# Second layer of an encoder trunk: two column blocks in the wide product form, and another timetable for the modulation sums

## The chip, the cores and the metric

The kernel runs on one core of one Trainium2 chip. The metric is the device time of one execution in microseconds (us); the time of a kernel is the median of its runs. Engines are called as the profile calls them: PE is TensorE's matmul, PEld its weight load, DVE is VectorE, ACT is ScalarE, POOL is GpSimd and SP is SyncE, which here only issues DMAs.

## What is computed

Two layers of a bidirectional encoder over one sequence of 256 tokens and 2048 features. Each layer is a parallel pair of attentions behind one input projection, one output projection, and a dense squared-ReLU MLP. Every sub-layer is modulated by a conditioning vector. Cut to what matters here:

```python
cond = silu(c)
for l in range(2):
    mod = cond @ w_ada[l] + b_ada[l]              # 2048 x 12288: six vectors of 2048
    sh_a, sc_a, g_a, sh_m, sc_m, g_m = split(mod, 6)
    h = rmsnorm(x) * (1 + sc_a) + sh_a
    proj = h @ w_in[l]                            # dq, dk, dv, cq, ckv, kr
    out_a = diff_attention(dq, dk, dv, ...)       # 4 heads, two score maps each
    q  = rmsnorm(cq, q_norm_g[l]) @ w_uq[l]       # latent queries, 512 wide
    kv = rmsnorm(ckv, kv_norm_g[l]) @ w_ukv[l]    # latent keys/values, 256 wide
    out_b = mla_attention(q, kv, rope(kr))        # 8 heads
    x = x + g_a * (concat(out_a, out_b) @ w_o[l])
    h = rmsnorm(x) * (1 + sc_m) + sh_m
    x = x + g_m * (square(relu(h @ w_mlp_in[l])) @ w_mlp_out[l])
return rmsnorm(x, final_norm_g)
```

## The kernel before

**Products.** Nearly every product is computed on two rounded parts of each operand, `hi` and `lo = value - hi`, both 32-bit "fp32r", as hi·hi + hi·lo + lo·hi. Activations are held transposed, a tile of 128 features by 256 tokens for each of the 16 k-tiles of `h`. Weights come in "raw" tiles of 128x2048 floats (1 MB) over SP's queue into a ring of five buffers (`raw`, L170). `weights` (L136) then makes two halves of each: ACT copies a half to `hi` (L151) and DVE subtracts to get `lo` (L154), each into a ring of four 128x1024 buffers.

There are two forms of the product of one weight tile (128x128) with one k-tile of `h`, called a unit here:

- the narrow form, `mac` (L191): three matmuls of 256 columns, weights hi, hi, lo (lines 194, 197, 198). `tile_cols` (L200) does a whole column tile of 16 units that way, `by_k` (L247) a block of tiles k by k, where several output banks stay open.
- the wide form: the hi and lo parts of `h` lie side by side, so that one matmul of 512 columns does hi·hi and hi·lo in the two halves of a bank, and one matmul of 256 columns adds lo·hi. `wides` (L207) does a pair of column tiles: all hi matmuls of both tiles (L217), then all lo matmuls of both (L220). `wide_by_k` (L265) does it k by k with open banks (L281 lo, L284 hi); at k = 0 it takes the lo matmul first. The two halves of a bank have then to be added: `joined` (L1344) calls `join` (L1350) for each of two banks, one ACT copy of 256 columns (L1351) and one DVE multiply-add (L1352), where the narrow form needs one ACT copy of 512 columns (`copy`, L344).

**The modulation sums.** `mod = cond @ w_ada` isn't done on PE. The matrix comes in 192 tiles of 1 MB over the same SP queue and the same five `raw` buffers (`ada_load`, L361), and DVE multiplies each tile with `cond` and adds along the row in one instruction (`ada_sums`, L375, L380), followed every second tile by an add of the bias (L392 or L394). When they are done is a timetable: each call of `weights` ends in `more_ada` (L159), which first issues the sums of tiles loaded since, behind that call's last `lo`, then adds `self.rate` to a credit and issues one load for each whole unit of credit. The rate is set by stage: constants `RATE_...` at L98. So a load issued in one call of `weights` has its sum in the next call. What a stage needs at the latest is done by force (`ada_need`). The last group, `g_m` of layer 1, is needed by `gate(1, 5)` (L1255) behind the first of the four blocks of the last MLP.

**The second layer's attention** (`layer`, L867, with `l = 1`): `norm_then_by_k` (L729) makes `h` and, with it, the six latent column tiles (cq, ckv) in `wide_by_k`, six banks open. Then, in the order of the code: the `w_d` block (four tiles: first diff-attention key head, last query head) by `by_k` in two banks `later`; six query tiles `w_q1` in three calls of `wides`; the latent keys' norm (`latent`, L713: squares on ACT, row sums and spread on PE, scale and split); copies of the two `later` banks to `kk` and `q`; the rope keys (`keys`, one narrow tile); six key tiles `w_t` by `tile_cols`, one by one (`col`, L909), with the latent queries' norm after the first of them and the scores of heads 0 to 2 (`probs`) between; then `up_r`, `up_k`, `up_q` (products with the latents, narrow), `up_v`, eight value blocks (`val`) between the eight MLA heads, and the output projection `w_o`.

**The last MLP** (`block_by_seven`, L1065): for each of four blocks of 2048 hidden features, a loop over pairs `m` of column tiles. Each pair is two single wide tiles, joined, through squared ReLU and split; from the third pair of a block on, each pair also runs two steps of an earlier pair (`seven`, L1133: `five` and `two`), products by sums and differences of weight blocks that DVE makes (L1164 to L1166, then L154). In block 0 the first six tiles were made with the norm, so the loop starts at m = 6. Steps that are left run after the loop; then the rest of the output columns (`rows_by_k`, L311 to L314).

The order of the instructions on each engine is made by the framework's scheduler from the order of the code, its dependences and its own cost estimates; `behind` fixes an order where the author wants one.

Of the kernel before, what the change touches and what calls it, by code (L numbers as in the profile page):

```python
# [16 lines left out]
P = 128  # L17
T = 256
D = 2048
NK = D // P  # L20
# [30 lines left out]
V_QG = 196  # L51
# [43 lines left out]
WHOLE = 6  # L95


RATE_A0, RATE_V, RATE_A1, RATE_A2, RATE_K, RATE_K1, RATE_M = 1.1, 1.6, 0.5, 0.7, 0.6, 0.0, 0.7  # L98
FILL = "0|1|2|3||||rlm"


class Trunk:
# [607 lines left out]
            ins = nc.vector.scalar_tensor_tensor(lo, t[:, i], sh[:, c], hi.bitcast(F32), ALU.add, ALU.subtract)  # L710
        return out, ins

    def latent(self, vals, g):  # L713

        nc = self.nc
        acc = None
        for v in vals:
            acc = self.sumsq(acc, v)
        r = self.rstd(acc, 2 * P * len(vals))
        out = []  # L720
        for b, v in enumerate(vals):
            t = self.t("lt")
            for i in range(2):
                k = 2 * b + i
                nc.vector.scalar_tensor_tensor(t[:, i], v[:, i], g[:, k : k + 1], r, ALU.mult, ALU.mult)
            out += self.split(t, "lat")
        return out
# [139 lines left out]
    def layer(self, l, acc=None):  # L867
        nc, io = self.nc, self.io
        qs = 1.0 / math.sqrt(128.0)
        ms = 1.0 / math.sqrt(192.0)  # L870
        fill = self.fills() if l == 0 else []
        later = []

        def next_by_k(kqs):
            def f(h, whole=()):
                if not later:
                    later.extend(self.open_banks(2))
                for kq in kqs:
                    f32 = whole if 4 * kq + 4 <= len(whole) else None
                    blocks = self.by_k_weights([io["w_d"][l, kq]], 4, f32)  # L880
                    self.by_k(later, blocks, h, 4 * kq, NK, 4, f32)
            return f

        if l == 0:
            early = {p: next_by_k(kqs) for p, kqs in EARLY.items()}
            h, banks = self.first_norm_then_by_k(acc, io["w_a"], 3, fill, early)
        else:
            self.rate = RATE_K1
            h, banks = self.norm_then_by_k(l, 0, 1, io["w_a1"])
            nc.gpsimd.dma_start(self.row, self.bias_kept)  # L890
        done = sum(len(k) for k in EARLY.values()) if l == 0 else 0
        self.rate = RATE_A0 if l == 0 else RATE_A1
        if l == 0:
            cqr = [self.copy(ps, "cqr") for ps in banks[:2]]
            ckr = self.copy(banks[2], "ckr")
        else:
            cqr = [self.joined(banks[i : i + 2], self.u("cqr")) for i in (0, 2)]
            ckr = self.joined(banks[4:], self.u("ckr"))
        q = []
        cq, ckv = [], []  # L900
        kk, qn, kn, qr, vm, a, at, v, o = [], [], [], [], [], [], [], [], []
        self.mo = []

        def keys():
            ps = self.bank("pkr")
            self.tile_cols(ps[:, 0], io["w_kr"][l], h)
            self.kr = (self.rope_k_parts if l else self.rope_k)(ps[:, 0])

        def col(i, out, scale):  # L909
            def f():  # L910
                if i % 2 == 0:
                    self.ps = self.bank("ps")
                self.tile_cols(self.ps[:, i % 2], io["w_t"][l, i], h)
                if i % 2:
                    out.append(self.copy(self.ps, "k", scale))
            return f
# [21 lines left out]
        def val(cg, kq):  # L938
            def f():
                if kq == 0:  # L940
                    self.pv = [self.bank("pv") for _ in range(2)]
                w = self.weights(io["w_dv"][l, cg, kq])
                w = [[z[:, 512 * j : 512 * j + 512] for z in y] for y in w for j in range(2)]
                self.tokens_by_k(self.pv, w, h[4 * kq : 4 * kq + 4], kq == 0, kq == 3)
                if kq == 3:
                    v.append([self.copy(ps, "v").rearrange("p a b -> p (a b)") for ps in self.pv])
            return f

        def probs(hd):
            return lambda: a.append(self.diff_probs(l, hd, q[hd], kk[hd]))  # L950
# [7 lines left out]
        for i in range(HM + 2):  # L958
            for s in range(3):
                if 0 <= i - s < HM:  # L960
                    mla.append(heads[i - s][s])
        next_by_k(range(done, 4))(h)
        if l == 0:
            q += [self.copy(ps, "q", qs) for ps in banks[3:]]
        else:
            for i in range(0, 6, 2):
                q.append(self.joined(self.wides([io["w_q1"][i + j] for j in range(2)], h), self.u("q"), qs))
        ckv += self.latent([ckr], self.vec[:, V_KVG + 2 * l : V_KVG + 2 * l + 2])
        kk.append(self.copy(later[0], "k", -1.0))
        q.append(self.copy(later[1], "q", qs))  # L970
        keys()
        order = [(0, kk, -1.0), (2, kk, -1.0), (4, kk, -1.0)]
        for n, (i, dst, scale) in enumerate(order):
            col(i, dst, scale)()
            if n == 0:
                cq += self.latent(cqr, self.vec[:, V_QG + 4 * l : V_QG + 4 * l + 4])
            probs(n)()
            col(i + 1, dst, scale)()
        if l:
            self.rate = RATE_A2  # L980
        vals = [val(cg, kq) for cg in range(2) for kq in range(4)]
        if l:
            up_r()
# [19 lines left out]
        turn(3)()  # L1003
        for f in mla[3:6]:
            f()
        if l == 0:
            self.rate = RATE_V
        self.interleave(
            vals,
            mla[6:] + [av[0][0], av[1][0]],  # L1010
        )
        if l == 0:
            self.rate = RATE_A0
        self.gate(l, 2)
        pss = [self.bank("pr") for _ in range(2)]
        self.rows_by_k(pss, self.weights(io["w_o"][l, 0, 0]), self.mo, 0)
# [14 lines left out]
        h, banks = self.norm_then_by_k(l, 3, 4, io["w_m0"] if l == 0 else io["w_m01"])  # L1031
# [613 lines left out]
```

## Time and profile before

| | |
|---|---|
| median of 3 runs | 2152.89 us (2151.78 to 2153.81) |
| profiled execution, its own time | 2149.43 us |
| span of its instructions | 2147.6 us |
| busy PE / PEld / DVE / ACT | 2119.8 / 1839.3 / 1776.0 / 1209.4 us |
| mean granted PE clock | 0.999 |
| second layer's attention, by the trace | about 1085 to 1444 us |
| its stretch from `w_d` to the last `w_t` tile | 1147.23 to 1251.74 us |
| last MLP, block 0, loop and remaining steps | 1482.9 to 1563.1 us |

The profile shows one execution of this kernel. The times that it gives lie inside the span; the profiled execution's own time is 1.8 us longer than the span. A matmul's duration in a row includes its way through the array and overlaps with the next one: what a matmul costs in a stream is the distance from its start to the next start. "Busy" is the time in which at least one instruction of that engine was under way.

### The profile page before, as it was taken

How to read it: one execution, taken by the hardware profiler on the slowest of the kernel's cores; microseconds unless marked ns; L12 is line 12 of the kernel's file. 1: busy time of each engine (PE TensorE's matmuls, PEld its weight loads, DVE VectorE, ACT ScalarE, POOL GpSimd, SP SyncE). 2: the span in 40 equal slices, each digit the busy share in tenths (PEclk: the TensorE clock that was granted, in tenths of full speed). 3: DMA queues.
4: the chain of work that ended last, by engine and by line, in shares of the span. 5: the costliest groups of instructions: out<-in, count | busy, mean ns of one | idle time of the engine just before them, and what ended most of it. 6: DMA issues, size and time to landing. Idle time of an engine off the chain costs nothing.

```text
span 2147.6 us, 29565 instructions
## 1 busy us (share of the span) xinstructions
PE 2119.8 (99%) x11411; PEld 1839.3 (86%) x11411; DVE 1776.0 (83%) x2444; ACT 1209.4 (56%) x1829; POOL 6.2 (0%) x18
## 2 busy tenths in 40 slices
PE   7999999999999999999999999999999999999998
PEld 5899888898888888888889998888888888888886
DVE  7889888988688888888877886778977897897897
ACT  6555663565465355345455576647645765664674
POOL 0000000000000000000000000000000000000000
PEclk9999999999999999999999999999999999999999
DMA  9998899799888988988967776775665564565553
GB/s 384 423 354 329 318 360 356 280 335 346 320 320 327 345 320 324 340 299 332 343 222 275 255 254 237 273 252 208 230 237 181 189 241 152 199 232 177 191 191 128
DMA packets 87245, 594.76 MB, mean 277 GB/s; under 512 B 9856, under 2 KB 10304, under 8 KB 20288
## 3 DMA queue, kind: packets, MB, share of 16 engines
q1 hardware_dynamic: 85968, 587.08, 73.8%
q0 software_dynamic: 848, 5.28, 0.6%
q8 instruction: 89, 1.46, 0.3%
q10 hardware_dynamic: 288, 0.52, 0.1%
q14 instruction: 52, 0.43, 0.1%
HBM read 589.66 MB, written 3.18 MB: 276 GB/s over the span
## 4 chain that ended last, share of the span: by engine, by line
PE 94%; DVE 3%; ACT 2%; DMA 1%; issue 1%; SPq 0%; ACTq 0%; DVEq 0%
PE ps L217 19%; PE pr L311 11%; PE pr L312 11%; PE pr L314 11%; PE ps L220 10%; PE pk L260 3%; PE pk L284 2%; PE pk L194 2%; PE pk L198 2%; PE pk L197 2%; PE pp L1156 2%; PE pp L1155 2%; PE pp L1157 2%; PE pv L298 2%; PE pv L296 2%; PE pv L297 2%
## 5 line engine op out<-in xcount | busy, mean ns | idle before, releaser
L151 ACT ACTIVATE hi<-raw 128x1024 fp32r<-128x1024 f32 (+2 forms) x714 | 719.7, 1019 | 617.1 <-PE pr L312 262.7
L154 DVE TENSOR_TENSOR lo<-raw,hi 128x1024 fp32r<-128x1024 f32 (+2 forms) x714 | 821.3, 1172 | 261.7 <-issue 104.8
L380 DVE SCALAR_TENSOR_TENSOR ada<-ada,cond 128x2048 f32<-128x2048 f32 x192 | 438.2, 2285 | 12.3 <-DMA ada<-in_w_ada 11.8
L217 PE MATMUL ps<-h,hi 128*128 128x512 f32 x1856 | 436.5, 390 | 0.0
L217 PEld LDWEIGHTS ps<-h,hi 128*128 128x128 f32 x1856 | 345.2, 188 | 71.0 <-DVE sum L1352 1.3
L311 PE MATMUL pr<-hi,hid 128*128 128x512 f32 x768 | 298.9, 389 | 0.0
L312 PE MATMUL pr<-hi,hid 128*128 128x512 f32 x768 | 298.8, 389 | 0.0
L220 PEld LDWEIGHTS ps<-h,lo 128*128 128x128 f32 x1856 | 234.1, 191 | 6.8
L220 PE MATMUL ps<-h,lo 128*128 128x256 f32 x1856 | 236.2, 283 | 0.0
L314 PE MATMUL pr<-lo,hid 128*128 128x512 f32 x768 | 190.3, 389 | 0.0
L314 PEld LDWEIGHTS pr<-lo,hid 128*128 128x128 f32 x768 | 144.2, 188 | 29.9
L311 PEld LDWEIGHTS pr<-hi,hid 128*128 128x128 f32 x768 | 144.2, 188 | 29.9
L312 PEld LDWEIGHTS pr<-hi,hid 128*128 128x128 f32 x768 | 144.2, 188 | 29.8
L1351 ACT ACTIVATE sum<-ps 128x256 f32<-128x256 f32 x110 | 41.9, 382 | 87.1 <-PE ps L220 86.2
L194 PE MATMUL pk<-h,hi 128*128 128x256 f32 x320 | 90.4, 285 | 0.2 <-ACT h L705 0.2
L198 PE MATMUL pk<-h,lo 128*128 128x256 f32 x320 | 90.5, 283 | 0.0
L197 PE MATMUL pk<-h,hi 128*128 128x256 f32 x320 | 90.5, 283 | 0.0
L260 PE MATMUL pk<-hf,w 128*128 128x256 f32 x384 | 84.1, 379 | 0.0
L260 PEld LDWEIGHTS pk<-hf,w 128*128 128x128 f32 x384 | 72.6, 190 | 10.4 <-ACT hf L677 0.6
L154 DVE TENSOR_TENSOR lo<-comb,hi 128x1024 fp32r<-128x1024 f32 x58 | 70.5, 1220 | 6.3 <-PE ps L220 6.3
L151 ACT ACTIVATE hi<-comb 128x1024 fp32r<-128x1024 f32 x58 | 60.7, 1053 | 8.5 <-PE pp L1157 5.5
L194 PEld LDWEIGHTS pk<-h,hi 128*128 128x128 f32 x320 | 61.2, 192 | 0.6 <-ACT h L705 0.5
(288 smaller groups left out, 3125.2 us busy)
## 6 DMA issues: line engine op xcount, KB each, us to landing
raw<-in_w_m SPq DMA_DIRECT2D x206, 1024.0 KB, 5.7
ada<-in_w_ada SPq DMA_DIRECT2D x192, 1024.0 KB, 6.2
raw<-in_w_o SPq DMA_DIRECT2D x32, 1024.0 KB, 5.8
raw<-in_w_ms SPq DMA_DIRECT2D x32, 1024.0 KB, 5.0
raw<-in_w_m SPq DMA_DIRECT2D x24, 768.0 KB, 5.1
raw<-in_w_dv SPq DMA_DIRECT2D x16, 1024.0 KB, 6.2
raw<-in_w_t SPq DMA_DIRECT2D x12, 1024.0 KB, 5.0
w<-in_w_a SPq DMA_DIRECT2D x24, 384.0 KB, 13.5
```

The costliest lines, as they stand in the source:

```text
L151: ins = self.nc.scalar.activation(hi, v, AF.Copy)
L154: ins = self.nc.vector.tensor_tensor(lo, v, hi.bitcast(F32), ALU.subtract)
L194: ins = mm(ps, hi, x[0], start=first, stop=False, skip_group_check=shared)
L197: mm(ps, hi, x[1], start=False, stop=False, skip_group_check=shared)
L198: self.last_mac = mm(ps, lo, x[0], start=False, stop=last, skip_group_check=shared)
L217: mm(ps.rearrange("p a b -> p (a b)"), part(w, k, 0), x[2], start=k == 0, stop=False)
L220: mm(ps[:, 0], part(w, k, 1), x[0], start=False, stop=k == nk - 1)
L260: self.nc.tensor.matmul(ps, v, whole[k], start=first, stop=last, skip_group_check=True)
L311: mm(ps, xh[:, c], part(i, 0), start=kq == 0 and i == 0, stop=False)
L312: mm(ps, xl[:, c], part(i, 0), start=False, stop=False)
L314: self.last_mm = mm(ps, xh[:, c], part(i, 1), start=False, stop=kq == 3 and i == 3)
L380: ins = nc.vector.scalar_tensor_tensor(w, w, 1.0, self.cond, ALU.mult, ALU.mult, accum_out=acc[:, i : i + 1])
```

## The change

Six edits, all for the second layer, whose core is shown below. (1) The `w_d` block goes behind the three `w_q1` pairs and takes `wide_by_k` over four open banks instead of `by_k` over two; its results are made by `joined`. (2) The six `w_t` tiles are done in pairs by `wides` and `joined`: `col(i)` does both tiles of a pair when `i` is even, and nothing when it is odd. (3) The squares and their sum for the latent queries' norm are split from `latent` into `squared` and issued ahead of `keys()`. (4) The rate of the modulation loads is 0.7 (was 0.5) for `w_q1` and `w_d`, 0.25 (was 0.5) for `keys` and `w_t`, 0 (was 0.7) for the `up_` products and the first value block, 1.0 (was 0.7) for the other seven value blocks and 0.6 (was 0.7) for `w_o`. The rates of the first layer, of the norms and of the MLPs stay as they are.

```diff
-RATE_A0, RATE_V, RATE_A1, RATE_A2, RATE_K, RATE_K1, RATE_M = 1.1, 1.6, 0.5, 0.7, 0.6, 0.0, 0.7
+RATE_A0, RATE_V, RATE_K, RATE_M = 1.1, 1.6, 0.6, 0.7
+RATE_K1, RATE_A1, RATE_C1, RATE_V1, RATE_O1 = 0.0, 0.7, 0.25, 1.0, 0.6
...
-    def latent(self, vals, g):
-
-        nc = self.nc
+    def squared(self, vals):
         acc = None
         for v in vals:
             acc = self.sumsq(acc, v)
-        r = self.rstd(acc, 2 * P * len(vals))
+        return acc
+
+    def latent(self, vals, g, acc=None):
+
+        nc = self.nc
+        r = self.rstd(acc or self.squared(vals), 2 * P * len(vals))
...
         def col(i, out, scale):
             def f():
+                if l:
+                    if i % 2 == 0:
+                        ps = self.wides([io["w_t"][l, i + j] for j in range(2)], h)
+                        out.append(self.joined(ps, self.u("k"), scale))
+                    return
...
-        next_by_k(range(done, 4))(h)
         if l == 0:
+            next_by_k(range(done, 4))(h)
             q += [self.copy(ps, "q", qs) for ps in banks[3:]]
         else:
             for i in range(0, 6, 2):
                 q.append(self.joined(self.wides([io["w_q1"][i + j] for j in range(2)], h), self.u("q"), qs))
+            later = self.open_banks(4)
+            for kq in range(4):
+                self.wide_by_k(later, self.by_k_weights([io["w_d"][l, kq]], 4, None), h, 4 * kq, NK)
         ckv += self.latent([ckr], self.vec[:, V_KVG + 2 * l : V_KVG + 2 * l + 2])
-        kk.append(self.copy(later[0], "k", -1.0))
-        q.append(self.copy(later[1], "q", qs))
+        if l == 0:
+            kk.append(self.copy(later[0], "k", -1.0))
+            q.append(self.copy(later[1], "q", qs))
+        else:
+            kk.append(self.joined(later[:2], self.u("k"), -1.0))
+            q.append(self.joined(later[2:], self.u("q"), qs))
+        acc = None
+        if l:
+            self.rate = RATE_C1
+            acc = self.squared(cqr)
         keys()
...
             if n == 0:
-                cq += self.latent(cqr, self.vec[:, V_QG + 4 * l : V_QG + 4 * l + 4])
+                cq += self.latent(cqr, self.vec[:, V_QG + 4 * l : V_QG + 4 * l + 4], acc)
             probs(n)()
             col(i + 1, dst, scale)()
         if l:
-            self.rate = RATE_A2
+            self.rate = 0.0
...
-        if l == 0:
-            self.rate = RATE_V
+        self.rate = RATE_V1 if l else RATE_V
         self.interleave(
...
-        if l == 0:
-            self.rate = RATE_A0
+        self.rate = RATE_O1 if l else RATE_A0
```

## Prediction, made before the changed kernel ran

> **What bounds the kernel now.** I read the page first, then its chain of waits, then the busy time by stretch, then the order of time.
>
> ```profile
> span 2147.6 us, 29565 instructions
> PE 2119.8 (99%) x11411; PEld 1839.3 (86%) x11411; DVE 1776.0 (83%) x2444; ACT 1209.4 (56%) x1829; POOL 6.2 (0%) x18
> PE 94%; DVE 3%; ACT 2%; DMA 1%; issue 1%; SPq 0%; ACTq 0%; DVEq 0%
> ```
>
> PE is busy for 99% of the span, and 94% of the chain that ends last is PE. So a change gains what it takes from PE's own stream, and loses whatever makes PE wait. Both have to be looked for in their stages.
>
> ```profile
> core 0: us, PE busy (x) PEld busy (x) DVE busy (x) ACT busy (x) POOL busy (x), PEclk, DMA share, GB/s
> 1147.23:1170.27 23.04, 23.04 (x195) 23.04 (x194) 16.02 (x19) 9.60 (x14) 0.00 (x0) 1.00 0.80 292
> 1170.27:1203.61 33.34, 33.34 (x195) 29.53 (x194) 21.23 (x24) 16.25 (x19) 0.00 (x0) 1.00 0.74 263
> 1210.69:1251.74 41.05, 41.05 (x327) 40.42 (x325) 36.41 (x77) 23.74 (x45) 0.00 (x0) 1.00 0.67 235
> ```
>
> These are `w_d` (narrow), `w_q1` (wide) and `w_t` (narrow) in the second layer's attention. PE never pauses in them, at full granted clock. So no wait is there to be removed: the edits can gain by a cheaper stream alone. DVE is at 70%, 64% and 89%.
>
> **The wide form: what it takes from PE.** The price of a matmul in a stream is the distance between starts.
>
> ```profile
> 1147.23 0.28 PE L194 MATMUL pk<-h,hi 128*128 128x256 f32 x1
> 1147.35 0.28 PE L197 MATMUL pk<-h,hi 128*128 128x256 f32 x1
> 1147.47 0.28 PE L198 MATMUL pk<-h,lo 128*128 128x256 f32 x1
> 1147.59 0.28 PE L194 MATMUL pk<-h,hi 128*128 128x256 f32 x1
> ...
> 1170.27 7.44 PE L217 MATMUL ps<-h,hi 128*128 128x512 f32 x32
> 1177.55 3.63 PE L220 MATMUL ps<-h,lo 128*128 128x256 f32 x29
> ...
> 1122.03 1.55 PE L284 MATMUL pk<-h,hi 128*128 128x512 f32 x6
> 1123.41 0.88 PE L281 MATMUL pk<-h,lo 128*128 128x256 f32 x6
> 1124.13 0.40 PE L284 MATMUL pk<-h,hi 128*128 128x512 f32 x1
> ```
>
> A narrow unit is three matmuls 0.12 us apart, 0.36 us; the 192 of `w_d` fill their 23.04 us exactly at that pace. In `wides`, 32 matmuls of 512 columns take 1177.55 - 1170.27 = 7.28 us, 0.2275 each; with 0.12 for the one of 256 columns a unit is 0.3475. (All 96 units of `w_q1`: 33.34 / 96 = 0.347.) In `wide_by_k`, six units take 1124.13 - 1122.03 = 2.10 us, 0.350 each. So the edit that looks like a third fewer matmuls saves 10 to 12.5 ns a unit. The six `w_t` tiles are 96 units: 96 x 0.0125 = 1.2 us. `w_d` is 64 units by `wide_by_k`: 64 x 0.010 = 0.6 us (0.8 at the pace of `wides`). Together 1.8 us off PE.
>
> The Trainium skill, page "TensorE: Matmul & The Clock Gate", section "Back-to-back issue gap", speaks against even that: a warm matmul of N columns follows the one before by N / 2.4 + 2.5 ns, so that three of 256 (328 ns) cost what one of 512 and one of 256 do (325 ns). By that rule the 160 units would save 0.4 us, and the sum below would be 4.9 instead of 3.5. The rows contradict it at 256 columns, with 120 ns, and the rows are used.
>
> **What else the attention part adds.**
>
> ```profile
> L1351 ACT ACTIVATE sum<-ps 128x256 f32<-128x256 f32 x110 | 41.9, 382 | 87.1 <-PE ps L220 86.2
> L1352 DVE SCALAR_TENSOR_TENSOR sum<-ps,sum 128x256 f32<-128x256 f32 x10 | 4.2, 418 | 0.1
> L346 ACT ACTIVATE k<-ps x6: 570/578/581, 179.2 to 1252.8; 128x512 f32<-128x512 f32 x6
> L154 DVE TENSOR_TENSOR lo<-raw,hi 128x1024 fp32r<-128x1024 f32 x27 | 32.5, 1219 | 4.7 <-ACT hi L151 4.7
> L380 DVE SCALAR_TENSOR_TENSOR ada<-ada,cond 128x2048 f32<-128x2048 f32 x192 | 438.2, 2285 | 12.3 <-DMA ada<-in_w_ada 11.8
> ```
>
> Five results are joined instead of copied: each is two ACT copies of 0.38 for one of 0.58 (+0.9 us of ACT in all) and two DVE additions of 0.42 (+4.2 us of DVE). By the timetable (below) `w_t` and `keys` lose two modulation sums of 2.29 us, so DVE there goes from 36.41 by -4.6 + 2.5 to about 34.3 of some 39.8 us; `w_q1` with `w_d` goes from 37.25 by +4.6 + 1.7 to 43.5 of some 55.8. Both stay below PE, and I cost the joins at nothing. If that cover were gone, it would be 0.84 us a join.
>
> The moves: `w_d`'s four loads pass `w_q1`'s six on SP's queue, all of 1 MB into the same ring, so nothing is late by it. The squares of the latent queries (two ACT squares, one DVE addition) go ahead of `keys`; PE's row sums that wait for them come behind a whole pair, 11.1 us, and cost nothing more than before. `probs(1)` and `probs(2)` find their keys a pair earlier. One place is tight: in a pair the `lo` buffers come free only with the second half of the stream (1177.55 + 8 x 0.12 = 1178.5, 8.2 us into 11.1), and `wide_by_k` starts with a `lo`. A subtraction of 1.22 ends at 9.5 if DVE is free and at 11.8 behind a sum: 0 to 0.7 us, once. I take 0, because in the wide stretch above DVE is free for a third of the time.
>
> **The timetable: what moves where.** Counting the calls of `weights` through the first layer (27 at 1.1, 8 at 1.6, 14 at 0.6, 114 at 0.7) gives 130.7, so the second layer starts with a credit of 0.7; the trace has 30 loads left then, two of them in the MLP:
>
> ```profile
> L364 SPq DMA_DIRECT2D ada<-in_w_ada x30: 327/328/328, 1129.7 to 1475.9; - x30
> L364 SPq DMA_DIRECT2D ada<-in_w_ada x2: 327/328/328, 1469.0 to 1475.9; - x2
> ```
>
> The count agrees: 0.7 + 17 x 0.5 + 27 x 0.7 = 28.1, so 28 in the attention. With the new rates: 0.7 + 10 x 0.7 + 7 x 0.25 + 6 x 0 + 7 x 1.0 + 14 x 0.6 = 24.85, so 24, and six are left for the MLP. There the credit runs 0.85 + 0.7n: loads at calls 1, 2, 4, 5, 6 and 8, sums at calls 2, 3, 5, 6, 7 and 9, where they were at 3 and 4. Calls 2 to 9 are the second tile of m = 6 to the first of m = 14, all in block 0's loop. The attention is relieved of four sums where PE didn't wait anyway, and the MLP gets four more. What is DVE's room there?
>
> ```profile
> 1484.60:1492.50 7.90, 7.90 (x46) 6.90 (x45) 5.93 (x13) 7.56 (x16) 0.00 (x0) 1.00 0.43 140
> 1492.50:1525.90 33.40, 33.40 (x190) 29.35 (x189) 32.76 (x54) 24.37 (x40) 0.00 (x0) 1.00 0.65 251
> 1525.90:1549.00 23.10, 23.10 (x122) 19.88 (x121) 21.91 (x30) 15.75 (x22) 0.00 (x0) 1.00 0.40 143
> 1549.00:1563.10 14.10, 14.05 (x70) 11.32 (x69) 14.07 (x21) 11.29 (x18) 0.50 (x1) 1.00 0.82 292
> ```
>
> Hardly any. From the place of call 2's sum to the end of the loop's products DVE works 5.93 + 32.76 + 21.91 + 14.07 = 74.67 of 78.5 us: 3.83 idle. And in the chain of waits that stretch isn't PE's:
>
> ```profile
> 1524.88 0.97 PE ps L220 x8
> ...
> 1525.94 1.23 DVE lo L154
> ...
> 1557.68 1.15 DVE lo L154
> 1558.87 0.50 PE pp L1156
> ```
>
> From 1525.94 to 1558.87 the chain runs through DVE alone but for 1.5 us of ACT and some issue, and where it hands back, PE has begun to wait:
>
> ```profile
> PEld pp L1156 <- DVE lo L154: 0.5, 1, 0.5
> ```
>
> So the lead that DVE had is used up at the end of the loop, and what is added before comes out as PE's wait. Four sums are 4 x 2.29 = 9.16 us; against 3.83 of idle time 5.3 us are over. Bounds: if all sums ahead of 1525.9 go into lead that PE doesn't miss, only call 9's is left, 2.3; if none of the idle time can be filled, 9.2. I take 5.3, as DVE's idle pieces lie at both ends of the sums' places. Behind the sums on DVE's queue stand the subtractions for PE's next tiles and for `five` and `two`; PE waits for those.
>
> **Sum.** -1.8 + 5.3 = +3.5 us, with its own range of 2.3 - 1.8 = +0.5 to 9.2 - 1.8 = +7.4. The rows are from the profiled execution, 2149.43 us, which is 3.46 below the median of the runs; it would become 2152.9, and the median 2152.89 + 3.5 = 2156.4 (2153.4 to 2160.3).
>
> **Rivals.** First, only the saving: the scheduler lets a sum wait while other work is ready, and DVE's work spreads beyond the loop, where it has 40.45 of 55.9 us busy:
>
> ```profile
> 1563.10:1619.00 55.90, 55.90 (x248) 46.31 (x247) 40.45 (x46) 22.61 (x22) 0.55 (x1) 1.00 0.66 244
> ```
>
> Then -1.8, 2151.1. For it: two sums stood in that loop before, and PE had one wait of 0.5. Against it: the steps' own differences and subtractions can't be put off, since the products behind them close the block.
>
> Second, clearly slower: the ring of five raw buffers. A modulation tile holds its buffer from its load to the end of its sum:
>
> ```profile
> 1475.91 0.33 SPq L364 DMA_DIRECT2D ada<-in_w_ada  x1
> 1498.77 2.28 DVE L380 SCALAR_TENSOR_TENSOR ada<-ada,cond 128x2048 f32<-128x2048 f32 x1
> DMA to landing us min/median/max: 4.7/5.3/10.2
> ```
>
> That was 25 us. Two held at a time leave three buffers for two tiles, a step's blocks and their differences per pair. It decides when a weight tile's load is issued less than 5.3 + 1.22 us and ACT's conversion before PE wants it; then a landing of 5.3 comes on top: +8.8, 2161.7. Against it: a late DVE also gives the loads time.
>
> Third, the wide form gives nothing, if PEld, full in the narrow stretch (23.04 of 23.04), is no limit there and the distance is only the form of the stream: +5.3, 2158.2. Against it stand 96 wide units at 0.347; this is also the case nearest to the skill's rule.
>
> **How the numbers follow.** Forecast 0.50, only the saving 0.25, the ring 0.15, no gain of the form 0.06, something that none of these rows shows and that is faster 0.04. About 0.2% (4.3 us) is what a measurement of this kernel can tell from no change. The saving alone lies within it; of the forecast's own range I put 0.33 within and 0.17 beyond; ring and no gain lie beyond. So faster 0.04, same 0.58, slower 0.38. The range goes from 2150.3, just below the saving alone, to 2160.3, the forecast's upper bound, and leaves out the ring and the unknown.
>
> **What would show it.** Right: `w_d` takes 22.4 and three `w_t` pairs 33.3 us without their inserts; six modulation loads after 1424 instead of two; DVE without idle time from about 1490 to the loop's end and that loop some 5 us longer, with PE's waits on `lo` (L154). Wrong: a loop as long as before with six sums in it, PE waits in `w_q1` or `w_d`, or a pace of units other than 0.35.

## The result, and the profile after

The changed kernel takes 2159.34 us (median of 9 runs, 2157.08 to 2161.39) against 2152.16 for the kernel before (9 runs): ratio 1.0034, 95% interval 1.0025 to 1.0043. That is 7.2 us slower (5.4 to 9.3), where 3.5 slower was forecast. The profiled execution of the changed kernel took 2159.23 us.

The head of its page, to be read against the first fence of the prediction:

```profile
span 2157.2 us, 29275 instructions
PE 2121.5 (98%) x11251; PEld 1830.5 (85%) x11251; DVE 1780.8 (83%) x2454; ACT 1208.7 (56%) x1834; POOL 6.2 (0%) x18
PE 90%; DVE 5%; ACT 2%; DMA 2%; issue 1%; SPq 0%; ACTq 0%; DVEq 0%
```

PE has 160 matmuls less, one for each of the 160 units, but four points less of the chain are PE's. The busy time by stretch says where. First the kernel before, from its norm to the first `up_` product, from there to the last MLP, and block 0's loop to its last `pp` product:

```profile
1147.23:1251.74 104.51, 104.51 (x771) 100.07 (x769) 80.14 (x129) 52.78 (x84) 0.00 (x0) 1.00 0.74 261
1251.74:1482.90 231.16, 230.92 (x1224) 199.14 (x1222) 174.78 (x266) 143.53 (x260) 1.05 (x2) 1.00 0.71 251
1482.90:1562.87 79.97, 79.92 (x428) 68.66 (x426) 75.55 (x115) 59.83 (x95) 0.50 (x1) 1.00 0.59 219
```

The same three stretches of the changed kernel, with `w_q1` and `w_d` by themselves ahead (after the length come PE, PEld, DVE, ACT and POOL busy, the granted clock, the DMA share and GB/s):

```profile
1149.09:1182.43 33.34, 33.34 (x194) 29.52 (x193) 25.68 (x33) 16.68 (x25) 0.00 (x0) 1.00 0.80 290
1182.43:1204.88 22.45, 22.45 (x130) 19.63 (x129) 17.78 (x18) 8.09 (x9) 0.00 (x0) 1.00 0.92 343
...
1149.09:1251.67 102.58, 102.58 (x611) 91.50 (x609) 82.19 (x128) 52.10 (x83) 0.00 (x0) 1.00 0.73 265
1251.67:1483.05 231.38, 231.14 (x1224) 199.23 (x1222) 168.33 (x267) 143.88 (x266) 1.05 (x2) 1.00 0.67 233
1483.05:1572.01 88.96, 83.37 (x429) 69.36 (x427) 84.70 (x126) 59.79 (x95) 1.05 (x2) 0.98 0.69 242
```

The stretch with the edits is 1.93 us shorter, without a pause of PE. The middle, from the `up_` products to the MLP, is 0.22 longer. The loop is 8.99 us longer: DVE works 9.15 us more in it, and its idle time is what it was, 88.96 - 84.70 = 4.26 against 79.97 - 75.55 = 4.42. The rest from the loop's end is 0.46 longer (2157.2 - 1572.01 against 2147.6 - 1562.87). The changed kernel enters the first stretch 1.86 us later, though none of the edits acts before there; that is a difference between two executions (over the first 100 us the granted clock is 0.95 in the one and 1.00 in the other). The five terms make the 9.60 between the spans; without the 1.86 they make 7.74, which goes with the 7.2 of the medians.

What the changed kernel's PE and PEld wait for in the loop, from the list of waits (total, times, longest):

```profile
PE pp L1174 <- DVE lo L155: 3.8, 5, 1.5
PE pp L1173 <- ACT hi L152: 1.6, 1, 1.6
PEld pp L1174 <- DVE lo L155: 6.2, 7, 1.9
PEld pp L1173 <- ACT hi L152: 2.6, 2, 2.1
```

And the chain of waits there, in order of time:

```profile
1503.56 1.93 PE ps L221 x16
1506.35 1.13 DVE comb L1182
...
1516.25 2.21 DVE ada L381 x2
...
1522.27 2.21 DVE ada L381 x2
...
1531.15 0.50 PE pp L1174
...
1543.98 1.14 DVE comb L1182
...
1548.07 1.14 DVE lo L155
1549.25 0.51 PE pp L1174
```

From 1505.5 on the chain runs through DVE, now with modulation sums (L381) in it, and where PE picks it up, at 1531.15 and 1549.25, it comes out of a wait. (In the changed kernel L154 has become L155, L1155 and L1156 are L1173 and L1174, and L1164 is L1182.)

### The profile page after: what moved, and what is told of

Same layout as the page of the kernel before. It is cut to its first block, busy times and chain, and to the rows that moved or that the text cites. A ratio compares the mean times of both kernels' runs of the same rounds, so it can differ in the third digit from the quotient of the medians.

```text
span 2157.2 us, 29275 instructions
## 1 busy us (share of the span) xinstructions
PE 2121.5 (98%) x11251; PEld 1830.5 (85%) x11251; DVE 1780.8 (83%) x2454; ACT 1208.7 (56%) x1834; POOL 6.2 (0%) x18
## 4 chain that ended last, share of the span: by engine, by line
PE 90%; DVE 5%; ACT 2%; DMA 2%; issue 1%; SPq 0%; ACTq 0%; DVEq 0%
PE ps L218 19%; PE pr L312 10%; PE pr L315 10%; PE pr L313 10%; PE ps L221 10%; PE pk L261 3%; PE pk L285 3%; PE pp L1174 2%; PE pp L1175 2%; PE pp L1173 2%; PE pv L299 2%; PE pv L297 2%; PE pv L298 2%; PE pk L195 1%; PE pk L199 1%; PE pk L282 1%
## 5 line engine op out<-in xcount | busy, mean ns | idle before, releaser
L155 DVE TENSOR_TENSOR lo<-raw,hi 128x1024 fp32r<-128x1024 f32 (+2 forms) x714 | 821.4, 1172 | 269.2 <-issue 108.1
L218 PE MATMUL ps<-h,hi 128*128 128x512 f32 x1952 | 459.8, 390 | 0.0
L381 DVE SCALAR_TENSOR_TENSOR ada<-ada,cond 128x2048 f32<-128x2048 f32 x192 | 438.1, 2284 | 11.8 <-DMA ada<-in_w_ada 11.3
L218 PEld LDWEIGHTS ps<-h,hi 128*128 128x128 f32 x1952 | 363.4, 188 | 75.0 <-DVE sum L1370 1.3
L221 PEld LDWEIGHTS ps<-h,lo 128*128 128x128 f32 x1952 | 246.1, 191 | 7.0
L221 PE MATMUL ps<-h,lo 128*128 128x256 f32 x1952 | 248.2, 283 | 0.0
L155 DVE TENSOR_TENSOR lo<-comb,hi 128x1024 fp32r<-128x1024 f32 x58 | 70.4, 1220 | 5.8 <-PE ps L221 5.8
L195 PE MATMUL pk<-h,hi 128*128 128x256 f32 x256 | 72.3, 285 | 0.2 <-ACT h L706 0.2
L199 PE MATMUL pk<-h,lo 128*128 128x256 f32 x256 | 72.4, 283 | 0.0
L198 PE MATMUL pk<-h,hi 128*128 128x256 f32 x256 | 72.4, 283 | 0.0
L285 PE MATMUL pk<-h,hi 128*128 128x512 f32 x256 | 67.6, 394 | 0.0
```

Of the source, the lines that this page charges most:

```text
L155: ins = self.nc.vector.tensor_tensor(lo, v, hi.bitcast(F32), ALU.subtract)
L195: ins = mm(ps, hi, x[0], start=first, stop=False, skip_group_check=shared)
L199: self.last_mac = mm(ps, lo, x[0], start=False, stop=last, skip_group_check=shared)
L218: mm(ps.rearrange("p a b -> p (a b)"), part(w, k, 0), x[2], start=k == 0, stop=False)
L221: mm(ps[:, 0], part(w, k, 1), x[0], start=False, stop=k == nk - 1)
L285: ins = mm(ps, part(j, 0), both, start=False, stop=False, skip_group_check=True)
```

## The experiments

In what follows "loop" is the third stretch above. Its end is a little loose: the scheduler puts some row products (`rows_by_k`), 0.23 us each, ahead of the last `pp` product, none before, one in the changed kernel, three in some kernels below. Counted on to the next block's first tile, the loop is 140.03 before and 148.80 in the changed kernel, 8.77 more; the expectations from "All sums early" to "Number or place" and the one of the last experiment count it so. All medians stand beside the median of the kernel before in the same job. A ratio can differ from the quotient of the two medians by up to 0.0004.

**The wide form without its timetable.** The changed kernel with the old rates:

```diff
-RATE_K1, RATE_A1, RATE_C1, RATE_V1, RATE_O1 = 0.0, 0.7, 0.25, 1.0, 0.6
+RATE_K1, RATE_A1, RATE_C1, RATE_V1, RATE_O1 = 0.0, 0.5, 0.5, 0.7, 0.7
...
-            self.rate = 0.0
+            self.rate = 0.7
```

> The changed kernel with the old rates (0.5 up to the last key tile, 0.7 from there): wide form and earlier squares alone, two modulation sums left for the last MLP. Theory 'DVE time' (the loss is the DVE time of four more sums in block 0 of the last MLP, the gain is the cheaper PE stream): 1.9 us below the kernel before, block 0 as long as before (80 us from its first tile to its row products), the stretch from the first query tile to the last key tile 102.6 us. Theory 'raw ring' (the loss comes from buffers held by modulation tiles): the same here. If the wide form itself were to blame for any of the loss, this kernel would be above the kernel before.

2152.52 us (11 runs) against 2152.07, ratio 1.0006 (0.9997 to 1.0015): not the gain of 1.9. The stretch is 102.60 long and the loop 79.95, as expected; the gain is lost between them. By stretch and by PE's waits between 1250 and 1300:

```profile
1250.78:1483.93 233.15, 231.81 (x1224) 199.25 (x1223) 178.75 (x281) 144.09 (x266) 1.05 (x2) 1.00 0.71 254
```

```profile
PE pv L297 <- ACT kn L347: 0.6, 1, 0.6
PE pv L298 <- DVE lo L155: 0.5, 1, 0.5
```

The middle has 1.99 us more than before: at the first value block PE waits 1.1 us for ACT and DVE, and its weight loads (PEld) wait 1.9 us there, where neither waits in the kernel before. With the narrow `w_t` before it the old rates cost nothing there (231.16). So with the old rates the wide form gains nothing that can be told; it needs another timetable.

**The timetable without the wide form.** The kernel before with the new rates only:

```diff
-RATE_A0, RATE_V, RATE_A1, RATE_A2, RATE_K, RATE_K1, RATE_M = 1.1, 1.6, 0.5, 0.7, 0.6, 0.0, 0.7
+RATE_A0, RATE_V, RATE_A1, RATE_A2, RATE_K, RATE_K1, RATE_M = 1.1, 1.6, 0.7, 0.0, 0.6, 0.0, 0.7
...
+        if l:
+            self.rate = 0.25
...
+        self.rate = 1.0 if l else RATE_V
...
+        self.rate = 0.6 if l else RATE_A0
```

> The kernel before with the new rates alone: narrow form as before, six sums in the last MLP. Both theories: slower than before by the whole loss, 9 us, block 0 about 89 us. If the wide form were needed for the loss: no difference to before.

2161.26 us (5 runs) against 2152.07, ratio 1.0044 (1.0031 to 1.0057). Its loop:

```profile
1484.57:1572.18 87.61, 81.99 (x428) 68.15 (x427) 84.62 (x126) 59.70 (x95) 1.05 (x2) 1.00 0.68 246
```

The loss is the timetable's, all of it: +9.2 here without the saving of 1.9, +7.2 with it. It is in the loop: +7.64 there, with the full clock and DVE idle for 2.99. What of the six sums is it: DVE's time, or the raw buffers that they hold?

**The buffers without the time.** The changed kernel, whose last six sums cover 64 of 2048 columns (so the rest of these sums is left out); loads and buffers are the same:

```diff
+            n = 64 if (l, g) == (1, 5) and i >= NK - 6 else D
...
-                w, w, 1.0, self.cond, ALU.mult, ALU.mult, accum_out=acc[:, i : i + 1]
+                w[:, :n], w[:, :n], 1.0, self.cond[:, :n], ALU.mult, ALU.mult, accum_out=acc[:, i : i + 1]
```

> The changed kernel, with the last six modulation tiles loaded at the same places and held in the same buffers, but summed over 64 of their 2048 columns only (part of the last gate's sums is left out). 'DVE time': six sums cost 6 x 0.2 us instead of 6 x 2.3, PE's waits in block 0 vanish, block 0 is 80 us or a little less, total 2 us below the kernel before. 'Raw ring': the tiles are loaded as late and take buffers as before; block 0 stays some 5 us or more above 80, total 3 us or more above the kernel before.

2152.12 us (11 runs) against 2152.07, ratio 0.9999 (0.9990 to 1.0008). Its loop:

```profile
1483.68:1565.54 81.86, 80.90 (x431) 69.15 (x429) 72.26 (x125) 59.84 (x95) 0.50 (x1) 1.00 0.73 264
```

Six tiles in the ring, with DVE idle for 9.60 us, cost 1.89; 0.68 of that are three row products, and counted to the next block's first tile it is 1.21. Neither theory has this right: the buffers alone cost a little, far from 5.

**The time without the buffers.** All 30 tiles ahead of the MLP, and in the MLP six DVE instructions of the sums' length at the sums' places (`cond * 0 + cond`, which changes nothing):

```diff
-RATE_K1, RATE_A1, RATE_C1, RATE_V1, RATE_O1 = 0.0, 0.7, 0.25, 1.0, 0.6
+RATE_K1, RATE_A1, RATE_C1, RATE_V1, RATE_O1 = 0.0, 0.7, 0.25, 1.0, 1.0
...
+            if self.pad in (2, 3, 5, 6, 7, 9):
+                c = self.cond
+                self.behind(self.nc.vector.scalar_tensor_tensor(c, c, 0.0, c, ALU.mult, ALU.add), after)
```

> The changed kernel with all 30 modulation tiles of the second layer loaded and summed in the attention (rate 1.0 in the output projection), and in the last MLP, at the places of the six sums, six DVE instructions of the same length on a tile that lies in SBUF anyway (multiply by 0 and add, the value stays). No tile is loaded and no buffer of the ring held for them. 'DVE time': as slow as the changed kernel, 7 us above before, with the same PE waits on the subtractions in block 0. 'Raw ring': block 0 about 80 us, total 2 us below before.

2156.61 us (11 runs) against 2152.07, ratio 1.0020 (1.0012 to 1.0029). Its loop:

```profile
1483.29:1568.33 85.04, 81.21 (x428) 68.44 (x427) 84.01 (x117) 60.46 (x95) 1.05 (x2) 1.00 0.52 179
```

DVE's time alone costs 5.07 us in the loop, and here DVE is idle for 1.03 only: the idle time does get filled when no tiles are loaded for the sums. So DVE's time is the larger part of the loss, and not all of it. The rest is 2.57 up to the kernel with the rates alone (87.61) and 3.92 up to the changed kernel (88.96), whose clock fell (last section). The medians say the same: +4.5 here, +7.2 in the changed kernel. This rest comes with the tiles in the ring. What differs, two views of the traces show. First what SP issues and DVE starts in this kernel:

```profile
1522.33 0.33 SPq L177 DMA_DIRECT2D raw<-in_w_ms  x1
1534.52 0.33 SPq L177 DMA_DIRECT2D raw<-in_w_m  x1
...
1536.68 1.21 DVE L1189 TENSOR_TENSOR comb<-raw 128x1024 f32<-128x1024 f32 x1
1539.60 2.28 DVE L168 SCALAR_TENSOR_TENSOR cond<-cond 128x2048 f32<-128x2048 f32 x1
```

and in the changed kernel:

```profile
1522.33 0.33 SPq L365 DMA_DIRECT2D ada<-in_w_ada  x1
1524.51 0.33 SPq L171 DMA_DIRECT2D raw<-in_w_m  x1
1531.16 0.33 SPq L171 DMA_DIRECT2D raw<-in_w_ms  x1
...
1537.94 1.23 DVE L155 TENSOR_TENSOR lo<-raw,hi 128x1024 fp32r<-128x1024 f32 x1 [1.17 <-PE ps L221]
1539.59 2.28 DVE L381 SCALAR_TENSOR_TENSOR ada<-ada,cond 128x2048 f32<-128x2048 f32 x1
...
1543.90 1.22 DVE L1182 TENSOR_TENSOR comb<-raw 128x1024 f32<-128x1024 f32 x1
```

The two start 0.24 us apart at the loop and have kept step. At 1522.33 a buffer comes free in both; in the one it takes the weight tile of the next differences, in the other the sixth modulation tile, and the weight tile goes out 8.83 us later, behind another one (1524.51). The difference (`comb`, itself a user of a raw buffer) starts at 1536.68 in the one, ahead of the last sum, and at 1543.90 in the other, behind it; the changed kernel's DVE sits idle for 1.17 us ahead of the sum, and PE's wait for the subtraction behind the difference, 1.46 us up to 1549.25, follows.

But the late load is not what held the difference up. It landed 4.9 us after its issue, at 1536.1, before DVE's idle piece and 7.8 us before the difference. And none of the changed kernel's four larger idle pieces of DVE in the loop ends with a load: 1.17 and 1.39 us wait for PE's `ps` products (L221), 0.87 for ACT's `hi`, 0.62 for ACT's `relu`. What came late is the difference's place in DVE's order, which the scheduler fixes before the run. That it put it there because the tile gets its buffer later is likely, and not shown.

**All sums early.** The changed kernel with 1.0 for the last rate, nothing left for the MLP:

```diff
-RATE_K1, RATE_A1, RATE_C1, RATE_V1, RATE_O1 = 0.0, 0.7, 0.25, 1.0, 0.6
+RATE_K1, RATE_A1, RATE_C1, RATE_V1, RATE_O1 = 0.0, 0.7, 0.25, 1.0, 1.0
```

> The changed kernel with 1.0 instead of 0.6 for the last rate: all 30 modulation tiles of the second layer are loaded and summed before the MLP, none is left for block 0's loop. Theory 'the sums left for block 0's loop' (DVE's time and the buffers they hold): the saving of the wide form stays, -1.9 in the stretch from the norm to the first up_ product (102.6 us), the loop falls back to 140.0 us or a little under (its two sums of before are gone too, whose one wait was 0.5), and the time is 1.9 to 2.5 under before: about 2150. Rival 'the denser sums only move the trouble': fourteen sums at the w_o products instead of eight are too many there, PE waits between the up_ products and the MLP, 2.3 us for each sum that finds no room, and the time is 2152 or more.

2150.78 us (11 runs) against 2152.10, ratio 0.9996 (0.9988 to 1.0005). The last part of the attention to the MLP, and the loop:

```profile
1252.69:1483.99 231.30, 231.06 (x1224) 199.32 (x1222) 181.06 (x282) 143.58 (x266) 1.05 (x2) 1.00 0.73 264
1483.99:1564.55 80.56, 80.54 (x430) 68.83 (x429) 71.92 (x111) 60.40 (x95) 0.50 (x1) 1.00 0.50 179
```

The six sums cost nothing ahead of the MLP (231.30 against 231.38 with six fewer), the loop is back, and the stretch keeps its 102.58. So this version takes back the changed kernel's loss (-1.3 us against the kernel before in its job, where the changed kernel had +7.2 in its own); whether it beats the kernel before, the interval leaves open.

**Four left, and eight left**, by 0.75 and 0.45 for the same rate:

```diff
-RATE_K1, RATE_A1, RATE_C1, RATE_V1, RATE_O1 = 0.0, 0.7, 0.25, 1.0, 0.6
+RATE_K1, RATE_A1, RATE_C1, RATE_V1, RATE_O1 = 0.0, 0.7, 0.25, 1.0, 0.75
```

> The changed kernel with 0.75 for the last rate: four sums left for block 0's loop, two more than before, 4.6 us of DVE. Theory 'DVE's time': the six one-block instructions of the earlier run cost 4.9 in the loop for 13.7 us of work, the two sums of before 0: if what DVE can take in is one fixed sum of idle time, about 8.8 us of six, then four (9.2 us) cost 0.4: loop about 140.4, time -1.5 against before, about 2150.6. Theory 'ring of raw buffers on top': the buffers alone gave +1.2 for six tiles, and both together 8.8; for four tiles I expect half of what goes beyond DVE's time, 2 us: loop about 142.5, time about +0.5 against before.

2151.19 us (11 runs) against 2152.10, ratio 0.9997 (0.9988 to 1.0006).

```profile
1485.17:1566.57 81.40, 80.87 (x431) 68.95 (x430) 79.59 (x120) 60.12 (x95) 0.50 (x1) 1.00 0.66 240
```

> The changed kernel with 0.45 for the last rate: eight sums left for block 0's loop, 13.7 us of DVE more than before. Theory 'DVE's time': all idle time is used by then, each sum more than six costs its full 2.29: 4.9 + 4.6 = 9.5 in the loop (149.5 us), about +7.6 against before. Theory 'ring of raw buffers on top': 8.8 + 2 x 2.29 or more = 13.4 in the loop (153.4 us), about +11.5 against before. If the last tiles are summed after the loop's end, one sum less in either.

2161.26 us (5 runs) against 2152.10, ratio 1.0044 (1.0032 to 1.0057).

```profile
1484.05:1572.16 88.11, 82.75 (x427) 68.79 (x425) 86.20 (x127) 59.00 (x93) 0.00 (x0) 0.98 0.70 243
```

With four sums the loop has 1.43 more than before for 4.0 of DVE work; without its three row products, to the next block's first tile, it is 0.76 more, 140.79: nearer to DVE's time (140.4) than to the buffers' (142.5). With eight left, seven are in the loop and the eighth runs over its end; DVE is idle for only 1.91. To the next block it is 150.34, between DVE's time (149.5, or 147.2 with one sum less) and the buffers' (153.4, or 151.1), and a fall of the clock is in it (0.98): this kernel doesn't tell the two apart. So what the tiles add beyond DVE's time is no fixed price for a tile: nothing that can be told with four, 2.57 with six.

**Number or place.** With four left, all four stand in the loop's first half. Two kernels ask which counts: six, but at successive calls of `weights`, the last at call 7 and not 9; and four, but at calls 2, 4, 7 and 9.

```diff
-        self.rate = RATE_M
+        self.rate = 1.0 if l else RATE_M
```

> The changed kernel with a rate of 1.0 instead of 0.7 in the second layer's MLP: still six sums in block 0's loop, but one at each call, the last at call 7 instead of call 9, so about 17 us earlier in the loop. Theory 'number': six sums are 9.2 us of DVE more than before, wherever they stand: the loop stays at 148 to 149 us, time +7 against before. Theory 'place': the sums in the first half of the loop go into DVE's lead, the one late sum, for which DVE has no idle time left behind it and whose buffer the next difference waits for, makes most of the loss: loop 142 to 144 us, time 0 to +2 against before.

2158.35 us (6 runs) against 2151.66, ratio 1.0030 (1.0018 to 1.0041).

```profile
1484.10:1573.78 89.68, 85.40 (x431) 70.82 (x429) 84.67 (x125) 60.19 (x95) 0.50 (x1) 0.96 0.66 241
```

```diff
-RATE_K1, RATE_A1, RATE_C1, RATE_V1, RATE_O1 = 0.0, 0.7, 0.25, 1.0, 0.6
+RATE_K1, RATE_A1, RATE_C1, RATE_V1, RATE_O1 = 0.0, 0.7, 0.25, 1.0, 0.75
...
-        self.rate = RATE_M
+        self.rate = 0.4 if l else RATE_M
```

> The changed kernel with 0.75 for the last rate of the attention (four sums left) and 0.4 in the second layer's MLP, so that the four stand at calls 2, 4, 7 and 9 instead of 2 to 7. Theory 'number': as with four sums before, the loop is 140.8 us and the time 1 us under before. Theory 'place': the last two stand where the changed kernel's stood, and most of its loss is back: loop 144 to 148 us, time +2 to +6 against before.

2152.24 us (11 runs) against 2151.66, ratio 1.0003 (0.9994 to 1.0012).

```profile
1481.89:1564.40 82.51, 80.74 (x430) 69.15 (x429) 80.48 (x120) 60.84 (x95) 1.04 (x2) 1.00 0.67 237
```

"Place" falls: six early ones cost about as much as the changed kernel's (loop to the next block 149.06 against 148.80), and four with two late ones only 1.1 us more than four early ones. It is mostly the number. The place is not nothing: the six early ones had two falls of the clock in the loop (0.96), the changed kernel one. With 1.4 us for each fall (last section) taken off, an estimate, they are at 146.3 against 147.4.

**A held queue?** One thing more stood on SP's queue in the changed kernel: the load of the final norm's gain, which goes into the buffer of `cond` and waits for the last sum. SP's waits in the loop, and the rows of the two issues:

```profile
SPq L1235 <- DVE ada L381: 10.4, 1, 10.4
```

```profile
1541.91 0.33 SPq L1235 DMA_DIRECT2D cond<-in_fg  x1
1542.33 0.46 SPq L171 DMA_DIRECT2D raw<-in_w_m  x1
```

The weight tile behind it goes out 0.42 us after it. To tell this from the ring, that load was put on GpSimd's queue, in the changed kernel and in the kernel with DVE's time alone:

```diff
-            nc.sync.dma_start(fg, self.io["fg"].broadcast_to([P, D]))
+            nc.gpsimd.dma_start(fg, self.io["fg"].broadcast_to([P, D]))
```

> The changed kernel, whose load of the final norm's gain into the buffer of cond (1 MB) is issued on GpSimd's queue instead of SyncE's; nothing else is edited. In the changed kernel that load waited 10.4 us for the last modulation sum, at the head of SyncE's queue, and the weight tile behind it was issued at 1542.33, 0.4 us after it. Theory 'held queue': it is this that lets DVE sit idle in spite of its extra work; with the load elsewhere the weight tile goes out when its buffer is free, the loop falls from 89.0 to about 85 us (what DVE's time alone gave), time +3 to +4.5 against before. Theory 'ring of raw buffers': the tile has no free buffer any earlier, loop 88 to 89, time +7 as the changed kernel.

2158.52 us (8 runs) against 2152.56, ratio 1.0028 (1.0017 to 1.0038). SP's queue and the loop:

```profile
1531.28 0.33 SPq L171 DMA_DIRECT2D raw<-in_w_ms  x1
1535.78 0.33 SPq L171 DMA_DIRECT2D raw<-in_w_m  x1
```

```profile
1483.16:1572.09 88.93, 83.42 (x428) 69.34 (x427) 84.61 (x126) 59.81 (x95) 1.58 (x3) 0.98 0.69 242
```

> The earlier kernel with all 30 modulation tiles ahead of the MLP and six DVE instructions of 2.29 us in its place (they read cond, so that the gain's load waited 5.9 us for the last of them), with that load on GpSimd's queue. It shows DVE's time with neither buffers nor a held queue. Theory 'held queue': the tiles for the next pair were already out ahead of the gain's load there, so little changes: loop 84 to 85 us, time +4 against before. Theory 'ring of raw buffers': the same, 85.0. If the loop falls under 83, part of what was put down to DVE's time was the held queue too.

2156.83 us (11 runs) against 2152.56, ratio 1.0022 (1.0013 to 1.0031).

```profile
1481.83:1568.44 86.61, 82.77 (x428) 69.62 (x427) 84.10 (x117) 60.46 (x95) 1.58 (x3) 0.98 0.50 177
```

The tile goes out 6.55 us earlier, and the loop is the same to 0.03 us: the held queue costs the loop nothing. (The medians, +6.0 here and +7.2 in the changed kernel, come from two jobs and their intervals overlap. In the second kernel the loop is 1.57 longer than without the edit, which is PE's clock: last section.)

**The sums at the `up_` products.** The changed kernel with sums there again (0.7 at the `up_`, value and `w_o` products), two left for the MLP:

```diff
-RATE_K1, RATE_A1, RATE_C1, RATE_V1, RATE_O1 = 0.0, 0.7, 0.25, 1.0, 0.6
+RATE_K1, RATE_A1, RATE_C1, RATE_V1, RATE_O1 = 0.0, 0.7, 0.25, 0.7, 0.7
...
-            self.rate = 0.0
+            self.rate = 0.7
```

> The changed kernel with the sums given at the up_ products again (0.7 there instead of 0; 0.7 at the value and w_o products): two are left for the MLP, as before the change. Theory 'the sums at the up_ products delay the value products': PE waits about 2 us for DVE and ACT at the first value block, as it did with the old rates on the wide form: stretch 102.6, then +2.0, block 0's loop 140.0, time equal to before, about 2152.2. Rival 'it was the old rates in the key and w_t tiles that left DVE behind': no wait there, -1.9 altogether, about 2150.2.

2154.03 us (11 runs) against 2152.10, ratio 1.0009 (1.0000 to 1.0018).

```profile
1251.05:1486.12 235.07, 233.24 (x1224) 200.26 (x1222) 176.88 (x277) 143.93 (x266) 1.05 (x2) 0.99 0.69 247
```

PE's longest wait there:

```profile
PE pv L298 <- DVE lo L155: 1.6, 1, 1.6
```

The middle is 3.9 us longer than before. PE's wait for a subtraction at the first value block is 1.6 of it (the weight loads wait 2.3 there), and behind it seven starts lie 427 ns apart, 1.4 more (see the last section). So it is the sums at the `up_` products that cost the wide form its gain with the old rates; the changed kernel's rate of 0 there is right, and what was taken away there went to the wrong place.

## Why the prediction came out as it did

- **The saving: right.** 1.8 us were forecast, 1.93 came: `w_d` takes 22.45 us (22.4 forecast), and the stretch is 102.58. The rule of the Trainium skill (page "TensorE: Matmul & The Clock Gate", section "Back-to-back issue gap") would have had 0.4; that section gives it for an isolated matmul, and the measurement decides against it in this stream. With it the rival "no gain of the form" falls.
- **Joins and moves at nothing, and the `lo` hand-over at 0: right.** PE is busy for all of the 102.58 us.
- **The timetable: counted right.** Six modulation loads stand behind 1424, and the sums lie at the calls forecast. The row of the changed kernel:

```profile
L365 SPq DMA_DIRECT2D ada<-in_w_ada x6: 327/328/328, 1463.5 to 1522.3; - x6
```

- **DVE's room in the loop: the mechanism right, the term too small.** "Against 3.83 of idle time 5.3 us are over" took it that DVE's idle time would be filled. With DVE's time alone that is what happens: 5.07. In the kernel itself the idle time stayed (4.26, and 2.99 in the kernel with the rates alone, whose clock kept up), and "DVE without idle time" was wrong. The term came out at 8.99. In parts: 5.07 of DVE's time, 2.57 with the tiles in the ring, and about 1.4 of PE's clock, below; the last two are differences between single profiled executions.
- **The range holds the result partly by luck.** +3.5 was forecast and +7.2 came, twice as much. The upper bound takes it that none of the idle time can be filled; with DVE's time alone it is filled. That the number came near the bound all the same is the work of two things of which the sum has no term: the tiles' part, which stood as a rival outside the range, and the clock. The ring's 2161.7 is about as near to 2159.34 as the forecast's 2156.4.
- **The rival of the ring: a part of its size came, not by its way.** It was to come on top with 5.3, a landing that PE waits for; 2.57 came. Its place was right: tiles held, weight tiles issued 8.83 us later. But "a late DVE also gives the loads time" held at the place that was traced: the tile had landed 7.8 us before its difference, and what was late was the difference's place in DVE's order. With DVE idle for 9.60 the same tiles cost 1.21 to 1.89, and nothing with four sums that could be told apart. It was no other outcome beside the forecast; a part of it came together with the forecast's own term.
- **Only the saving: wrong**, as the kernel with the rates alone shows: the six sums stayed in the loop and PE waited.

What stays open: the six sums at successive calls left DVE 5.01 us idle, and with eight left only 1.91. Why DVE's order changes with the tiles was not shown, and one place only was traced. A ring of six buffers, or the difference held ahead of the last sum (with `behind`), would show whether buffers or order cost the 2.57; neither was tried.

## What to carry to other kernels

In this loop an off-path engine's work had no price by the instruction: it was nearly free until the stage was full, and cost its length or more from there. Four sums in the loop (DVE busy for 79.6 of 81.4 us) cost 0.8 us, six cost 9, of which DVE's time alone makes 5. So add up that engine's busy time against the stage's length, stage by stage, before work is moved. And count its idle time as room only with the engine's new order in view: the added tiles came with another order of loads and of DVE's work, and DVE stayed idle for 3.0 to 4.3 us where the same work without tiles left 1.0. Where such a timetable hangs on a few constants, the best one changes with the form of the products beside it: with the old rates the faster form lost its saving at the `up_` products, with the new ones in the last loop. With few or no sums at either place it kept it by the profile; the medians, 0.9 to 1.3 us under before, lie within what the intervals leave open.

## What the runs showed of the hardware

PE's clock fell for a few us behind waits of less than 2 us. In the changed kernel PE waited 1.46 us up to 1549.25; by stretch:

```profile
1483.05:1549.70 66.65, 63.09 (x341) 53.17 (x340) 63.96 (x99) 43.81 (x74) 0.00 (x0) 1.00 0.68 242
1549.70:1553.10 3.40, 3.40 (x10) 2.61 (x9) 3.30 (x4) 2.92 (x4) 0.00 (x0) 0.50 0.95 366
1553.10:1572.01 18.91, 16.88 (x82) 13.58 (x80) 17.44 (x25) 13.06 (x19) 1.05 (x2) 1.00 0.66 222
```

For 3.4 us the granted clock is 0.50: seven starts lie some 427 ns apart instead of 227, 7 x 0.2 = 1.4 us. It doesn't come with each such wait: an earlier one of 1.39 us in the same loop, up to 1530.01, left the clock at 1.00. The kernel with the rates alone had the same waits at the same places and kept its clock (1.00, loop 87.61). And of the two kernels with DVE's time alone, which have the same waits in the loop, the one that kept its clock,

```profile
1531.60:1535.00 3.40, 3.40 (x17) 2.77 (x16) 3.40 (x4) 2.36 (x3) 0.00 (x0) 1.00 0.00 0
```

ran 17 matmuls in the 3.4 us behind a wait, and the other 10:

```profile
1530.15:1533.55 3.40, 3.40 (x10) 2.65 (x9) 3.40 (x4) 1.29 (x2) 0.00 (x0) 0.50 0.00 0
```

The difference of their loops, 86.61 - 85.04 = 1.57, is mostly this. The Trainium skill, page "TensorE: Matmul & The Clock Gate", section "HAM oscillation — how this bites in real kernels", puts the rule as no pauses of PE over about 3.4 us; here pauses of 1.4 to 1.6 us were enough in some executions and not in others, and what decides it no run here shows.
